# A two-layer encoder kernel: order of the opening, a neighbourhood table laid out in full, and Hyena loads and PSUM reads moved

## The chip, the cores and the metric

One core of a Trainium2 chip runs the whole kernel in one launch. The metric is device time in microseconds (us) of one execution. PE is the matmul engine, DVE the vector engine, ACT the scalar engine, POOL the GpSimd engine, SP the engine whose queue issues most loads; ACT and POOL can issue transfers too.

## The reference

Input x is 512 tokens of 1024 channels, in float32, and so is the output. Each of two layers computes x + post_norm(mixer(pre_norm(x))) and then x + post_norm(ffn(pre_norm(x))), the norms being RMS norms:

```python
def rms_norm(x, gain):
    y = x * lax.rsqrt(jnp.mean(x * x, axis=-1, keepdims=True) + EPS)
    return y * gain
# mixer, layer 0: 8 heads of latent attention beside 8 heads of 2-D neighbourhood attention
#   s = q.k_window * scale + rpb[row_off][:, col_off];  p = softmax(s);  o = p.v_window
# mixer, layer 1: 4 heads of retention (forward and backward) beside 512 Hyena channels
#   z = dwconv3(u_proj);  x0, x1, v = split(z);  u = v * x1
#   y = irfft(rfft(u, 2L) * rfft(k_circ, 2L))[:L] + u * hy_bias;  out = y * x0
def conv_ffn(h, w_gate, w_up, conv_w, w_down):
    return (gelu(dwconv3(h @ w_gate, conv_w)) * (h @ w_up)) @ w_down
```

The neighbourhood table rpb is indexed by the offset between a query and each key of its 8 by 16 window; keys outside of the window take no part.

## The kernel before

**Arithmetic.** Activations lie channel-major: 8 tiles of 128 channels x 512 tokens. Every operand of a product is split into a high part in float32r and the rest (`split_to`, line 273: a cast on ACT, a subtraction on DVE or POOL), and `mm` (line 278) makes three matmuls of two parts each. A weight piece is 128 x 1024: `load_weight` (line 250) has SP load it to one of 2 `raw` buffers, ACT cast it to `whi` and DVE subtract to `wlo` (4 buffers each). `weight_ahead` keeps three pieces ahead of the one in use. PSUM has 8 banks in four tags: pj (2), A (3), B (2), C (1).

**Order.** The program is written in one order (`main`, line 522), and a planner then issues each engine's instructions by its own model of the times: of those that are ready in the model the first in program order goes first; `high_priority(n)` moves a block up by n places, and `issue_after(ins)` keeps a block behind `ins` on that instruction's engine. Each engine and each of the queues SP, ACT and POOL then runs its list strictly in order. A tile's memory is handed on when its last reader is done; a phase (l0, f0, l1, f1) takes over the memory of the one before, in the order in which its tags are first used.

**Opening.** 16 warm-up products of ones (line 528); SP loads x and the first four weight pieces in turn. Line 539 scales and splits x tile by tile (`scaled`, line 331), with a square on ACT (line 542) and a running sum on POOL (line 544) after each tile. `proj_tok` (line 476) makes the values of the neighbourhood heads: 8 steps over the channels, 12 matmuls each; before step 5 `stats` (line 286: sum over partitions on PE, then a power on POOL), before step 6 `spread` and a copy to `Rb`; `loads` (line 564) comes before step 7 and has SP load the column mask, the table rpb (8 x 384 columns, without mask) and the rope table. The four results are read from PSUM by ACT (line 598) and DVE (line 599).

**Neighbourhood heads, then latent heads.** `na0` (line 622) makes q and k and adds rpb and mask to three bias tiles per head (line 631, DVE); `na1` scores and softmax, `na2` transposes and values. `latent_kv` makes the rope part of the keys, kr (lines 728 to 731). `parts` (line 736), between the heads' last stages, splits kr three times into `kall` (line 746, ACT and POOL), which takes over the memory of rpb. Then `ml0`, `ml1`, `ml2` run pipelined.

**Boundary** (line 339): the output product, post norm, residual and next pre norm, in two halves of 256 tokens; the last four weight columns' products of the next stage run over the halves (`proj_halves`). Its two `stats` end in a power on POOL, and at its end `rcol`, spread to `Rb` (line 447).

**Layer 1.** The ffn of layer 0 also makes the Hyena filters (`filters`, line 963) and stores them to DRAM (`filt`, line 1004). `mixer1` (line 1061) stores x to DRAM (line 1065), has POOL load the forward transform's matrices (`dft_consts`, line 930), and runs `conv` for 12 projections through one tile `cv`: the first four read the products `pre` that the boundary left in PSUM. `spectrum` (line 1008) loads the filters back by ACT's queue, splits them and transforms them, in steps between the projections. The transform of u and the products with the filters follow (lines 1113 to 1143, chiefly DVE), then `proj_tok` for the retention values (read from PSUM by `scaled`, line 1149), three `gate` projections (line 1106, read by DVE), and the inverse transform (line 1162). `decays` (line 1040) is a chain of some 25 operations on 128 x 8 elements.

Of the kernel before, what the change touches and what calls it, by code (L numbers as in the profile page):

```python
# [16 lines left out]
P = 128  # L17
# [26 lines left out]
def shape_constants():  # L44
# [18 lines left out]

    mask = np.zeros((P, 3, 32, GR), np.float32)
    for typ, (q0, k0) in enumerate(((0, 0), (16, 8), (48, 32))):
        for p in range(P):
            col = q0 + p // GR
            st = min(max(col - 8, 0), GW - 16)
            kc = k0 + np.arange(32)
            mask[p, typ, (kc < st) | (kc >= st + 16), :] = -1.0e30  # L70
    c["namask"] = f32(mask.reshape(P, 3 * 256))
# [41 lines left out]
def lay_out(inp):  # L113
# [78 lines left out]

    r = np.pad(inp["a_rpb"][0], ((0, 0), (0, 0), (16, 16)))
    q = np.arange(P)
    r = r[:, 7 - (q % GR)[:, None, None] + np.arange(GR)[None, None, :], 15 - (q // GR)[:, None, None] + np.arange(48)[None, :, None]]
    a["rpb"] = f32(r.transpose(1, 0, 2, 3).reshape(P, MH * 384))
# [9 lines left out]
class Body:  # L206
    def __init__(self, ctx, tc, I, out, dbg=None):
# [10 lines left out]
        self.filt = self.dp.tile([2, S, HC], F32, name="filt")  # L218
        self.n = 0
        self.wi = 0  # L220
        self.wq = []
        self.cols = self.cp.tile([P, NCOL], F32, name="cols")
# [27 lines left out]
    def load_weight(self, n=1):  # L250
# [4 lines left out]
        for i in range(n):  # L255
            c = slice(i * 1024 // n, (i + 1) * 1024 // n)
            nc.sync.dma_start(raw[:, c], self.I["w"][self.wi][:, c])
            with self.tc.high_priority(WP):
                nc.scalar.copy(hi[:, c], raw[:, c])  # L259
                nc.vector.tensor_tensor(lo[:, c], raw[:, c], hi[:, c].bitcast(F32), ALU.subtract)  # L260
# [78 lines left out]
    def boundary(self, pool, tag, x, prod, gpost, gpre, ns, ftag, perm=False, rin=None):  # L339
# [104 lines left out]
        with self.tc.issue_after(self.last_mm):  # L444
            with self.tc.high_priority(HP):
                self.stats([acc2], D, out=self.rcol)
            nc.scalar.copy(self.Rb, self.spread(self.rcol, "C"))
# [74 lines left out]
    def main(self):  # L522
# [14 lines left out]
        with self.phase("l0") as p:  # L537
            acc = None
            for k in range(KT):
                self.scaled(h[k], x[k], self.col(C_MPRE + k), slice(0, S))  # L540
                sq = self.X("sq", tag="xb")
                nc.scalar.activation(sq, x[k], AF.Square)
                if acc is not None:
                    nc.gpsimd.tensor_tensor(acc, acc, sq, ALU.add)
                else:
                    acc = sq
            x, h, pre = self.mixer0(p, h, acc)
# [10 lines left out]
    def mixer0(self, p, h, acc):  # L558
        nc = self.nc
        mask = p.tile([P, 3 * 256], F32, name="namask")  # L560
        rope = p.tile([P, 2, S], F32, name="rope0")
        big = p.tile([P, MH, 384], F32, tag="big", name="rpb")

        def loads():
            nc.sync.dma_start(mask, self.I["namask"])
            for hd in range(0, MH, 2):
                nc.sync.dma_start(big[:, hd:hd + 2], self.I["rpb"][:, hd * 384:hd * 384 + 768].rearrange("p (a b) -> p a b", a=2))
            nc.sync.dma_start(rope, self.I["rope0"].rearrange("p (a b) -> p a b", a=2))
# [13 lines left out]
        def value_mm(ops, v, hd, pt, start, stop):  # L582
# [6 lines left out]
        pss = self.proj_tok(h, {7: loads, 5: lambda: self.stats([acc], D, out=self.rcol),  # L589
                                6: lambda: nc.scalar.copy(self.Rb, self.spread(self.rcol))})  # L590
# [31 lines left out]
        def na0(hd, _):  # L622
# [5 lines left out]
            b = p.tile([P, 2, 256], F32, tag="bias", bufs=2, name=self.nm("bias"))  # L628
            b = [b[:, 0], b[:, 1], self.X("bias", tag="xb")[:, :256]]
            for t, o in enumerate((128, 64, 0)):  # L630
                nc.vector.tensor_tensor(b[t], big[:, hd, o:o + 256], mask[:, t * 256:t * 256 + 256], ALU.add)
            return b
# [90 lines left out]
        def latent_kv():  # L723
# [8 lines left out]
            lat["kr"] = kr  # L732
# [3 lines left out]
        def parts():  # L736
# [7 lines left out]
            kall = p.tile([P, 6, S], F32R, tag="big", name="kall")  # L744
            for i in range(3):
                self.split_to(kall[64:128, 2 * i], kall[64:128, 2 * i + 1], lat["kr"][64:128], nc.gpsimd)
# [122 lines left out]
    def ffn(self, p, x, h, pre, l):  # L869
# [18 lines left out]
        for j in range(FT):  # L888
# [5 lines left out]
            nc.vector.tensor_tensor(t, gps, Rb, ALU.mult)  # L894
# [35 lines left out]
    def dft_consts(self, p, name):  # L930
        out = []
        for i, part in enumerate(("hi", "lo")):
            t = p.tile([P, 4, 2, 256], F32R, tag="dft" + part, name=name + part)
            self.nc.gpsimd.dma_start(t.rearrange("p m a b -> p (m a b)"), self.I[name][:, i * 2048:(i + 1) * 2048])
# [28 lines left out]
    def filters(self, new):  # L963
# [28 lines left out]
        for tk in range(4):  # L992
# [10 lines left out]
            for i, src in enumerate((t, n)):  # L1003
                nc.sync.dma_start(self.filt[i, ts], src)
# [3 lines left out]
    def spectrum(self, mats, at, kt, spec):  # L1008
        nc = self.nc
        for par in range(2):  # L1010
            for trig in range(2):
                m = 2 * par + trig
                sd = []
                for hh in range(2):
                    t = self.X("sd", tag="xb")
                    tk = 2 * par + hh
# [3 lines left out]
                for ft in range(2):  # L1020
                    ps = self.PS("C")
                    for hh in range(2):
                        c = slice(ft * P, ft * P + P)
                        self.mm(ps, (mats[0][:, m, hh, c], mats[1][:, m, hh, c]), sd[hh], hh == 0, hh == 1)
                    if par == 0:
                        t = self.X("sp", tag="xb")
                        nc.scalar.activation(t, ps, AF.Copy, scale=1.0 / 512)
                        spec[ft, trig] = t
                    else:
                        e, o, d = spec[ft, trig], kt(), kt()  # L1030
# [266 lines left out]
```

## Time and profile before

| | |
|---|---|
| median of 3 runs (each) | 1312.72 us (1308.06, 1312.72, 1312.88) |
| the profiled execution: time, span | 1307.53 us, 1305.8 us |
| PE busy (share of the span) | 1271.7 us (97%) |
| DVE, ACT, POOL busy | 813.9 (62%), 582.9 (45%), 80.9 us (6%) |
| mean granted clock of PE | 0.993 |

The span runs from the first to the last instruction. Busy time of an engine is the union of its instructions; an average over stages hides where an engine stands idle, so the stages are looked at one by one. The granted clock is the share of full speed that the throttle let PE have.

### The profile page before, as it was taken

To read this page: it belongs to the slowest core of one execution; us is meant where nothing else is said; L and a number is where in the kernel's file an instruction comes from. 1 tells how busy PE (TensorE), PEld (TensorE's weight loads), DVE (VectorE), ACT (ScalarE), POOL (GpSimd) and SP (SyncE) were. 2 spreads that over 40 slices of the span, in tenths; PEclk is the share of its full clock that TensorE was granted. 3 is DMA by queue.
4 is the path that set the end of the run, shared out by engine and by line. 5 is a ranking of instruction groups with operands and counts; after the bars stand their busy time and mean duration, and the time that the engine had idled before them with its cause. 6 is when DMAs were issued, how large, how long until landed. Compare 5 with 4: busy or idle time off the path is not lost.

```text
span 1305.8 us, 16380 instructions
## 1 busy us (share of the span) xinstructions
PE 1271.7 (97%) x6370; PEld 1057.5 (81%) x6370; DVE 813.9 (62%) x1298; ACT 582.9 (45%) x943; POOL 80.9 (6%) x73
## 2 busy tenths in 40 slices
PE   9999799999999999999999999999999999999997
PEld 7788677997888788888987878778988888888886
DVE  6679898478766665322588785774875555552223
ACT  5456798456533333222454245544653333332221
POOL 4021322000000000000000000000000000000002
PEclk9999899999999999999999989999999999999999
DMA  7222012223434333333264233214233333333331
GB/s 269 86 65 79 3 33 68 82 79 116 121 123 135 122 113 97 99 111 97 83 226 128 58 120 95 81 49 130 66 113 98 97 97 97 97 97 104 107 97 65
DMA packets 41563, 130.62 MB, mean 100 GB/s; under 512 B 4652, under 2 KB 6892, under 8 KB 40973
## 3 DMA queue, kind: packets, MB, share of 16 engines
q1 hardware_dynamic: 35868, 116.92, 29.0%
q10 hardware_dynamic: 5040, 8.45, 2.0%
q0 software_dynamic: 576, 4.19, 0.9%
q8 instruction: 50, 0.82, 0.3%
q14 instruction: 29, 0.23, 0.1%
HBM read 123.26 MB, written 6.29 MB: 99 GB/s over the span
## 4 chain that ended last, share of the span: by engine, by line
PE 87%; DVE 5%; ACT 3%; issue 2%; DMA 1%; POOL 1%; SPq 0%; DVEq 0%; POOLq 0%; ACTq 0%
PE pspj L280 17%; PE pspj L282 17%; PE pspj L281 17%; PE psA L280 10%; PE psA L282 10%; PE psA L281 10%; DVE wlo L260 1%; ACT e L794 1%; DMA raw<-in_w 1%; PE psB L292 1%; PE psB L671 1%; PE psB L810 1%; DVE h L334 1%; ACT whi L259 1%; PE psC L282 1%
## 5 line engine op out<-in xcount | busy, mean ns | idle before, releaser
L259 ACT CAST whi<-raw 128x1024 fp32r<-128x1024 f32 (+1 forms) x200 | 209.1, 1048 | 432.1 <-PE pspj L281 237.8
L260 DVE TENSOR_TENSOR wlo<-raw,whi 128x1024 fp32r<-128x1024 f32 (+1 forms) x200 | 246.6, 1235 | 204.8 <-ACT whi L259 202.8
L280 PE MATMUL pspj<-h,whi 128*128 128x512 f32 (+1 forms) x664 | 250.5, 377 | 2.8 <-DVE v L599 2.7
L281 PE MATMUL pspj<-h,whi 128*128 128x512 f32 (+1 forms) x664 | 249.6, 376 | 0.0
L282 PE MATMUL pspj<-h,wlo 128*128 128x512 f32 (+1 forms) x664 | 249.4, 376 | 0.0
L282 PE MATMUL psA<-h,wlo 128*128 128x512 f32 (+1 forms) x424 | 155.4, 367 | 0.7 <-DVE wlo L260 0.7
L280 PE MATMUL psA<-h,whi 128*128 128x512 f32 (+1 forms) x424 | 156.1, 368 | 0.0
L281 PE MATMUL psA<-h,whi 128*128 128x512 f32 (+1 forms) x424 | 155.1, 366 | 0.0
L280 PEld LDWEIGHTS pspj<-h,whi 128*128 128x128 f32 x664 | 125.5, 189 | 25.4 <-DVE v L599 3.1
L282 PEld LDWEIGHTS pspj<-h,wlo 128*128 128x128 f32 x664 | 125.4, 189 | 22.2
L281 PEld LDWEIGHTS pspj<-h,whi 128*128 128x128 f32 x664 | 125.5, 189 | 22.0
L280 PE MATMUL pspj<-ahi,whi 128*128 128x512 f32 x308 | 121.4, 394 | 0.0
L282 PE MATMUL pspj<-ahi,wlo 128*128 128x512 f32 x308 | 120.7, 392 | 0.0
L281 PE MATMUL pspj<-alo,whi 128*128 128x512 f32 x308 | 119.5, 388 | 0.0
L282 PEld LDWEIGHTS psA<-h,wlo 128*128 128x128 f32 x424 | 79.8, 189 | 15.5 <-DVE wlo L260 1.9
L280 PEld LDWEIGHTS psA<-h,whi 128*128 128x128 f32 x424 | 80.0, 189 | 14.8 <-issue 2.6
L281 PEld LDWEIGHTS psA<-h,whi 128*128 128x128 f32 x424 | 80.0, 189 | 12.4
L894 DVE TENSOR_TENSOR t<-psA,Rb 128x512 f32<-128x512 f32 x40 | 27.6, 691 | 83.4 <-PE psA L282 83.3
L282 PEld LDWEIGHTS pspj<-ahi,wlo 128*128 128x128 f32 x308 | 57.8, 188 | 13.5
L281 PEld LDWEIGHTS pspj<-alo,whi 128*128 128x128 f32 x308 | 57.8, 188 | 12.9
L280 PEld LDWEIGHTS pspj<-ahi,whi 128*128 128x128 f32 x308 | 57.9, 188 | 11.5
L299 POOL TENSOR_TENSOR r<-v,mhalf 128x2 f32<-128x2 f32 (+1 forms) x14 | 13.7, 977 | 847.7 <-DVE v L297 690.2
(360 smaller groups left out, 2140.1 us busy)
## 6 DMA issues: line engine op xcount, KB each, us to landing
raw<-in_w SPq DMA_DIRECT2D x198, 512.0 KB, 3.5
x<-in_xT SPq DMA_DIRECT2D x16, 256.0 KB, 4.8
fflt<-in_fwin SPq DMA_DIRECT2D x8, 256.0 KB, 2.9
xspill<-f ACTq DMA_DIRECT2D x8, 256.0 KB, 2.6
sd<-filt ACTq DMA_DIRECT2D x8, 256.0 KB, 3.3
x<-xspill ACTq DMA_DIRECT2D x8, 256.0 KB, 3.2
rpb<-in_rpb SPq DMA_DIRECT2D x4, 384.0 KB, 4.6
filt<-fs SPq DMA_DIRECT2D x4, 256.0 KB, 2.5
```

What stands on the lines that cost most here:

```text
L259: nc.scalar.copy(hi[:, c], raw[:, c])
L260: nc.vector.tensor_tensor(lo[:, c], raw[:, c], hi[:, c].bitcast(F32), ALU.subtract)
L280: nc.tensor.matmul(ps, stat[0], mov[0], start=start, stop=False)
L281: nc.tensor.matmul(ps, stat[0], mov[1], start=False, stop=False)
L282: self.last_mm = nc.tensor.matmul(ps, stat[1], mov[0], start=False, stop=stop).ins
L292: nc.tensor.matmul(ps[:, j:j + 1], a[:, j * P:(j + 1) * P], self.ones, start=a is accs[0], stop=a is accs[-1])
L299: self.pow = nc.gpsimd.tensor_tensor(r, v, self.mhalf[:, :c], ALU.pow)
L334: self.nc.vector.scalar_tensor_tensor(lo, src, g, hi.bitcast(F32), ALU.mult, ALU.subtract)
L671: tr = lambda o, i: nc.tensor.transpose(o, i, self.ident)
L794: nc.scalar.activation(e, ps, AF.Exp, bias=nmx, accum_out=den[:, i:i + 1])
L810: nc.tensor.transpose(pt[:, i * P:(i + 1) * P], es[i][:, j * P:(j + 1) * P], self.ident)
L894: nc.vector.tensor_tensor(t, gps, Rb, ALU.mult)
```

## The change

1. *Opening.* All eight tiles are scaled and split before the squares; the running sum goes from POOL to DVE; `stats` and the copy to `Rb` come one step later; 14 warm-up products instead of 16. The rope table is loaded by POOL's queue, in program order after `proj_tok`.
2. *Neighbourhood table.* The host lays rpb out with the mask in it (8 heads x 3 kinds x 256 columns, 3 MB in place of 1.5 MB and a mask of 0.4 MB); each head's bias tile (three buffers) is loaded by POOL's queue, and the additions on DVE are gone.
3. *kr* is split into `kall` where it is made; `kall` has memory of its own.
4. *Boundaries.* Casts of weight pieces that come later in the program stay behind the copy to `Rb` on ACT.
5. *Hyena.* The filters are split before they are stored (twice the bytes); POOL's queue loads the parts, all 16 tiles at once behind the matrices of the transform, whose load is put 300 places up; the tiles x0 come first in the phase's memory; the four products `pre` are read into x0 at once; x is stored to DRAM after the second `conv`; `decays` runs in the ffn before; the gate projections and the retention values are read from PSUM by ACT alone.

```diff
 opening (main), and mixer0
-            acc = None
             for k in range(KT):
                 self.scaled(h[k], x[k], self.col(C_MPRE + k), slice(0, S))
-                sq = self.X("sq", tag="xb")
-                nc.scalar.activation(sq, x[k], AF.Square)
-                if acc is not None:
-                    nc.gpsimd.tensor_tensor(acc, acc, sq, ALU.add)
...
+            sqs = [self.X("sq", tag="xb") for _ in range(KT)]
+            for k in range(KT):
+                nc.scalar.activation(sqs[k], x[k], AF.Square)
+                if k:
+                    nc.vector.tensor_tensor(sqs[0], sqs[0], sqs[k], ALU.add)
...
-            nc.sync.dma_start(mask, self.I["namask"])
...
-            nc.sync.dma_start(rope, self.I["rope0"].rearrange("p (a b) -> p a b", a=2))
+            nc.gpsimd.dma_start(rope, self.I["rope0"].rearrange("p (a b) -> p a b", a=2))
...
-            for t, o in enumerate((128, 64, 0)):
-                nc.vector.tensor_tensor(b[t], big[:, hd, o:o + 256], mask[:, t * 256:t * 256 + 256], ALU.add)
+            b = p.tile([P, 3, 256], F32, tag="bias", bufs=3, name=self.nm("bias"))
+            nc.gpsimd.dma_start(b, self.I["rpb"][:, hd * 768:hd * 768 + 768].rearrange("p (a b) -> p a b", a=3))
...
-            lat["kr"] = kr
+            for i in range(3):
+                self.split_to(kall[64:128, 2 * i], kall[64:128, 2 * i + 1], kr[64:128], nc.gpsimd)
 load_weight, boundary
+                with self.tc.issue_after(self.hold) if self.hold is not None else ExitStack():
+                    nc.scalar.copy(hi[:, c], raw[:, c])
...
+            self.hold = nc.scalar.copy(self.Rb, self.spread(self.rcol, "C")).ins
 ffn
+            if l == 0 and j == 4:
+                with self.tc.issue_after(scaled.ins):
+                    self.decay = self.decays(self.cp)
 filters, spectrum
-                nc.sync.dma_start(self.filt[i, ts], src)
+                hl = self.X("fh", F32R), self.X("fl", F32R)
+                self.split_to(*hl, src)
+                for part in range(2):
+                    nc.sync.dma_start(self.filt[part, i, ts], hl[part].bitcast(F32))
...
-                    nc.scalar.dma_start(t, self.filt[trig, tk * P:(tk + 1) * P])
-                    sd.append(at(trig))
-                    self.split_to(*sd[-1], t)
+                    with self.tc.high_priority(300), self.tc.issue_after(self.consts):
+                        nc.gpsimd.dma_start(parts[m][hh][part], self.filt[part, m % 2, tk * P:(tk + 1) * P])
 mixer1
-        for k in range(KT):
-            nc.scalar.dma_start(spill[k * P:(k + 1) * P], x[k])
-        mats = self.dft_consts(p, "dftf")
+        x0 = [p.tile([P, S], F32, name=f"x0{j}") for j in range(4)]
+        with self.tc.high_priority(300):
+            mats = self.dft_consts(p, "dftf")
...
+        for j in range(4):
+            scaled(pre[j], x0[j])
...
+            if j == 1:
+                with self.tc.issue_after(self.taken):
+                    for k in range(KT):
+                        nc.scalar.dma_start(spill[k * P:(k + 1) * P], x[k])
...
-            g, ps = self.X("rg", tag="xb"), self.proj(h)
-            nc.vector.tensor_tensor(g, ps, Rb, ALU.mult)
+            g = self.X("rg", tag="xb")
+            nc.scalar.copy(g, self.proj(h))
+            nc.vector.tensor_tensor(g, g, Rb, ALU.mult)
...
+            t = self.X("rv", tag="xb")
+            nc.scalar.activation(t, ps, AF.Copy, scale=rcol[:, j:j + 1])
             rv.append(two("t1"))
-            self.scaled(rv[-1], ps, rcol[:, j:j + 1], slice(0, S))
+            self.split_to(*rv[-1], t)
...
-        lg = self.decays(p)
+        lg = self.decay
```

## Rows read from the trace of the kernel before

**Rows 1.** The page, busy time of each engine, its share of the span, instructions.

```profile
PE 1271.7 (97%) x6370; PEld 1057.5 (81%) x6370; DVE 813.9 (62%) x1298; ACT 582.9 (45%) x943; POOL 80.9 (6%) x73
```

**Rows 2.** Four stretches: length, PE, PEld, DVE, ACT, POOL busy, PEclk, DMA share, GB/s.

```profile
35.00:165.00 130.00, 123.17 (x639) 99.53 (x638) 104.36 (x204) 73.93 (x168) 24.76 (x18) 0.97 0.19 57
...
128.00:154.00 26.00, 19.20 (x91) 14.36 (x92) 21.32 (x45) 16.56 (x43) 8.78 (x7) 0.87 0.07 20
...
296.00:640.00 344.00, 344.00 (x1547) 280.85 (x1547) 189.81 (x272) 128.88 (x160) 0.70 (x1) 1.00 0.36 111
...
766.00:780.00 14.00, 10.99 (x45) 9.08 (x44) 11.87 (x17) 5.13 (x8) 0.00 (x0) 0.76 0.37 114
```

**Rows 3.** Timeline of PE in the opening: start, length, line, operands, idle before it.

```profile
0.93 6.51 PE L528 MATMUL psC<-ones 128*128 128x128 f32 x32 [0.93 <-DVE ones L226]
...
19.61 0.50 PE L281 MATMUL pspj<-wlo,h 128*128 128x512 f32 x1 [1.03 <-DVE wlo L260]
...
34.69 0.50 PE L280 MATMUL pspj<-h,whi 128*128 128x512 f32 x1 [2.71 <-DVE v L599]
```

**Rows 4.** Timeline of ACT, DVE and POOL in the opening.

```profile
31.67 1.05 ACT L259 CAST whi<-raw 128x1024 fp32r<-128x1024 f32 x1 [3.49 <-DMA raw<-in_w]
...
7.49 0.75 DVE L334 SCALAR_TENSOR_TENSOR h<-x,cols,h 128x512 fp32r<-128x512 f32 x1
...
12.12 5.20 DVE L334 SCALAR_TENSOR_TENSOR h<-x,cols,h 128x512 fp32r<-128x512 f32 x3
...
11.63 9.08 POOL L544 TENSOR_TENSOR sq<-sq,sq 128x512 f32<-128x512 f32 x5 [0.52 <-ACT sq L542]
```

**Rows 5.** Timeline of SP's queue in the opening.

```profile
12.60 0.43 SPq L565 DMA_DIRECT2D namask<-in_namask  x1
...
19.59 0.33 SPq L257 DMA_DIRECT2D raw<-in_w  x1
```

**Rows 6.** Loads of line 257 issued between 668 and 690, issue to landing.

```profile
DMA to landing us min/median/max: 3.5/4.5/6.8
```

**Rows 7.** Timeline from 118 to 141: ACT, POOL, DVE and PE.

```profile
133.53 1.66 ACT L274 CAST kall<-kr 64x512 fp32r<-64x512 f32 x3
...
134.22 3.76 POOL L275 TENSOR_TENSOR kall<-kr,kall 64x512 fp32r<-64x512 f32 x3 [9.52 <-ACT kall L274]
...
118.07 0.61 DVE L665 TENSOR_SCALAR ebuf<-ebuf,rd 128x256 f32<-128x256 f32 x2
...
131.46 0.41 DVE L631 TENSOR_TENSOR bias<-rpb,namask 128x256 f32<-128x256 f32 x1
...
139.28 1.68 DVE L665 TENSOR_SCALAR ebuf<-ebuf,rd 128x256 f32<-128x256 f32 x2
...
139.41 0.48 PE L671 MATMUL psB<-ident,s 128*128 128x128 f32 x2 [2.99 <-DVE s L665]
```

**Rows 8.** Timeline at the head of layer 1: POOL and PE.

```profile
645.50 1.08 POOL L299 TENSOR_TENSOR r<-v,mhalf 128x2 f32<-128x2 f32 x1 [8.04 <-DVE v L297]
...
670.48 0.76 POOL L934 DMA_DIRECT2D dftfhi<-in_dftf  x1 [23.91 <-ACT t L274]
...
680.10 0.50 PE L282 MATMUL psC<-t,dftflo 128*128 128x512 f32 x1 [2.24 <-DMA dftflo<-in_dftf]
...
698.64 0.50 PE L1101 MATMUL psB<-ident,u 128*128 128x128 f32 x2 [1.26 <-DVE u L1090]
```

**Rows 9.** Line 275 on POOL, head outputs: count, ns min/median/max, first and last start.

```profile
L275 POOL TENSOR_TENSOR a<-at,a x15: 1270/1295/2142, 68.0 to 223.8; 64x512 fp32r<-64x512 f32 x15
```

**Rows 10.** Timeline from 765 to 775: ACT, DVE and PE.

```profile
765.03 0.69 ACT L333 ACTIVATE t<-pspj,rcol 128x512 fp32r<-128x512 f32 x1 [1.79 <-PE pspj L282]
...
773.41 0.74 DVE L334 SCALAR_TENSOR_TENSOR t<-pspj,rcol,t 128x512 fp32r<-128x512 f32 x1
...
769.45 0.38 PE L280 MATMUL psA<-dftihi,t 128*128 128x256 f32 x1 [1.78 <-ACT t L274]
...
774.54 0.63 PE L280 MATMUL pspj<-h,whi 128*128 128x512 f32 x1
```

More of the change, by code (lines that the diff above doesn't have):

```diff
@@ L194, in lay_out @@
     q = np.arange(P)
-    r = r[:, 7 - (q % GR)[:, None, None] + np.arange(GR)[None, None, :], 15 - (q // GR)[:, None, None] + np.arange(48)[None, :, None]]
-    a["rpb"] = f32(r.transpose(1, 0, 2, 3).reshape(P, MH * 384))
+    t = np.full((P, MH, 3, 32, GR), -1.0e30, np.float32)
+    for typ, (q0, k0) in enumerate(((0, 0), (16, 8), (48, 32))):
+        col, kc = q0 + q // GR, k0 + np.arange(32)
+        off = (16, 8, 0)[typ] + np.arange(32)
+        e = r[:, 7 - (q % GR)[:, None, None] + np.arange(GR)[None, None, :], 15 - (q // GR)[:, None, None] + off[None, :, None]]
+        st = np.minimum(np.maximum(col - 8, 0), GW - 16)[:, None]
+        near = (kc[None, :] >= st) & (kc[None, :] < st + 16)
+        t[:, :, typ] = np.where(near[:, None, :, None], e.transpose(1, 0, 2, 3), t[:, :, typ])
+    a["rpb"] = f32(t.reshape(P, MH * 768))
     fw = np.zeros((P, 64 + 64 + 64 + 1024), np.float32)
@@ L588, in mixer0 @@
         self.new_factor()
-        pss = self.proj_tok(h, {7: loads, 5: lambda: self.stats([acc], D, out=self.rcol),
-                                6: lambda: nc.scalar.copy(self.Rb, self.spread(self.rcol))})
+        pss = self.proj_tok(h, {6: lambda: self.stats([acc], D, out=self.rcol),
+                                7: lambda: nc.scalar.copy(self.Rb, self.spread(self.rcol))})
+        loads()
         rcol, Rb = self.rcol, self.Rb
@@ L627, in na0 @@
                 pair[hd // 2] = q, qk_tile(kn)
[L628 to L632 removed]
+            b = p.tile([P, 3, 256], F32, tag="bias", bufs=3, name=self.nm("bias"))
+            nc.gpsimd.dma_start(b, self.I["rpb"][:, hd * 768:hd * 768 + 768].rearrange("p (a b) -> p a b", a=3))
+            return [b[:, t] for t in range(3)]
         def na1(hd, bias):
@@ L1084, in mixer1 @@
                               lambda: p.tile([P, S], F32, tag="t2", bufs=8, name=self.nm("ks")), ks)
-        u, x0 = [], [p.tile([P, S], F32, name=f"x0{j}") for j in range(4)]
+        next(steps)
         for j in range(4):
-            u.append(conv(8 + j, p.tile([P, S], F32, name=f"u{j}")))
+            scaled(pre[j], x0[j])
+        u = []
+        for j in range(4):
+            u.append(conv(8 + j, p.tile([P, S], F32, name=f"u{j}"), x0[j]))
+            if j == 1:
+                with self.tc.issue_after(self.taken):
+                    for k in range(KT):
+                        nc.scalar.dma_start(spill[k * P:(k + 1) * P], x[k])
         for j in range(4):
@@ L1264 @@
 WP = 5
-WARM = 16
+WARM = 14
 LATE = 7
```

88 lines of the change are left out of this document (38 added, 50 removed).

## The prediction

> **What bounds the kernel now.** The page comes first: PE is busy for 97% of the span and no other engine for more than 62% [rows 1]. The kernel is bound by its matmuls, and the change removes none of them but two warm-ups. What can be won is the 34 us in which PE stands idle, and the time in which it runs at the lower of its clocks. So I asked next for busy time by stretches. In the ffn of layer 0 PE is busy for 344.00 of 344.00 us [rows 2]: whatever the change puts there costs nothing while DVE (189.81) and ACT (128.88) have room. Between 35 and 165 us PE loses 6.83 us, and nearly all of it (6.80) between 128 and 154 [rows 2]. Between 766 and 780 it loses 3.01 us more. In both stretches the granted clock falls, to a mean of 0.87 and 0.76; elsewhere it is 1.00. Then I read the timelines where PE waits: the opening [rows 3, 4], the passage from neighbourhood to latent heads [rows 7], the head of layer 1 [rows 8] and the gates [rows 10].
>
> **Opening.** PE waits 1.03 us for a low part of a weight at 19.61 and 2.71 us at 34.69 for the values to be read from PSUM [rows 3]. The first wait comes from DVE: its split takes 0.75 us alone, but three take 5.20 while POOL's sums run (five in 9.08) [rows 4]. With the sums on DVE that stretching ends. The second wait is that ACT, due to read PSUM, stood 3.49 us at a weight still in flight [rows 4], issued behind the tables on SP's queue [rows 5]; without tables there it comes earlier. Two warm-ups fewer are 4 of 32 records in 6.51 us, so 0.8 us [rows 3]. Together up to 4.5 us. Late next would be the second weight piece. For the tables do not stay behind: the planner issues what is ready. The mask left SP at 12.60, the fifth weight piece at 19.59, though that piece comes first in the program [rows 5]. Rope and the first three bias tiles wait for nothing, and POOL has nothing else to do, so I expect those four loads (1.7 MB by their shapes) within the first 5 us, beside x and the first weights. Beside 2.1 MB that POOL loaded in layer 1 a weight took up to 6.8 us to land, where the quickest took 3.5 [rows 6]. So 1.7 MB delay a piece by 3.3 x 1.7 / 2.1 = 2.7 us. I take 2.0 us as the gain; the ends are 4.5 (no collision) and -0.9 (two pieces delayed).
>
> The Trainium skill, "DMA: Bandwidth & Descriptors", section "Issuing engines are not separate DMA queues", says that transfers run on the same 16 engines and interleave whichever engine issued them, so that another queue saves only the issuing time. By that rule the tables would push the loads back by their whole volume and the opening would win about nothing: a median of 1299.7 instead of the 1297.7 below. The delay in rows 6 agrees in kind; a queue to queue share is not shown by any row.
>
> **Neighbourhood table.** 24 additions at 0.41 us [rows 7], 9.8 us of DVE, go. They lie where PE waits for nothing but the stretch counted next: nothing. The eight loads on POOL's queue wait for the tile three heads back; what is queued behind them is POOL's splits of head outputs, wanted only at the output product. Nothing.
>
> **kr.** Between 128 and 154 the late chain is softmax, transposes, PE. ACT spends 1.66 us on three casts of kr in its middle, and POOL's 3.76 us of subtractions beside it stretch two products on DVE from 0.61 to 1.68 [rows 7]. Both leave the stretch: 1.66 + 1.07 = 2.7 us off the wait of 2.99 at 139.41. With that wait gone PE should keep its clock; 0.13 x 26 = 3.4 us of full speed were lost [rows 2], part of it in idle time, so I count 2.3. Sum 5.0, ends 0 (another order of ACT brings the wait back) and 9.1 (all idle time and the clock). Where kr is made now, before 128, PE has no wait to lengthen.
>
> **Boundaries.** The casts held back are of pieces that have no free buffer before the copy anyway: nothing either way, within half a us.
>
> **Head of layer 1.** POOL's load of the transform stood until 670.48, and PE waited 2.24 us for it at 680.10 [rows 8]. The matrices' memory was that of the boundary's sums. With the x0 tiles in front they take over split activations, dead when the last down product ends, which is before the power at 645.50 [rows 8], so this wait goes. DVE loses eight splits and the `decays` chain in this stretch, ACT eight casts and a change of tables; the wait of 1.26 for u [rows 8] should shrink. I count 2.24 + 0.8 = 3.0. Ends: 4.3 (both waits and the idle of the first part) and -2.0 for the new: 18 loads now stand in POOL's queue at the very time of the boundary's two powers, the first at 645.50 [rows 8]. Two issues ahead of a power cost 2 x 0.76 us. The moved splits and `decays` land in the ffn under its 344 us of PE; if that cover were gone they would cost eight splits at about 0.74 us (the nearest row, [rows 10]) and the small chain, some 10 us. The stores of x leave ACT's queue where nothing waits for them. Nothing.
>
> **Values and gates.** At 765.03 ACT reads the first value bank, DVE at 773.41 only, as its products with the filters stand in front [rows 10]. So the first gate's matmul comes at 774.54, and PE takes inverse transforms instead, whose inputs are late (1.78 us at 769.45 and more) [rows 10]. Read by ACT alone the bank is free near 766, a gate follows at once, and three gates of 24 matmuls each give DVE time to catch up. The idle 3.0 us and the lost clock, 0.24 x 14 = 3.4 us [rows 2], make 6.4. I take 5.0, as ACT gets four casts and three copies more; ends 0 and 6.4, below nothing by 1 if ACT falls behind.
>
> **Sum.** 2.0 + 5.0 + 3.0 + 5.0 = 15.0 us. The profiled execution took 1307.53 us for a span of 1305.8, so it would take 1292.5. The runs' median stands 5.2 us higher, at 1312.72; the same gain puts it at 1297.7.
>
> **Rivals.**
> - *The planner puts the inverse transform first again.* It works with model times, and nothing forces gates first. For it: it did so before. Against it: in the model too the bank is free sooner. That term is 0, and the time 1302.7.
> - *The waits pass on.* DVE is busy for 21.32 of 26 us around the passage and 11.87 of 14 us at the gates [rows 2]. If it is the next to be late, two thirds of the gains come back as other waits: 5 us are left, 1307.7. Nearly no change.
> - *POOL's queue becomes the path.* At the boundary before layer 1 all 18 loads are ready when the last down product ends, shortly before the power at 645.50. If they go first, the power waits 18 x 0.76 = 13.7 us, or, stretched beside DVE as POOL's subtractions were (2142 against 1270 ns) [rows 9], 23 us. The second half of the products hangs on that power through spread, update and splits, with little to cover it, so PE would stand some 22 us. Against it: the power has a place of higher rank than the loads. It decides when more than some ten issues get in front. The other terms are 12, so the time is 1312.7 + 22 - 12 = 1322.7: slower.
>
> The Trainium skill, "SBUF — State Buffer", section "SBUF: two separate sides", warns that POOL cannot write descriptors while DVE runs an operation that takes their shared port pair, so that a load issued by POOL looks blocked by DVE; with its figure of about 3.1 us in place of 0.62 us, 18 issues would be an estimated 56 us. No row here shows such an issue.
>
> **How the numbers follow.** Two runs of this kernel differ by less than about 0.5% (6.6 us) with nothing changed; faster is below 1306.1, slower above 1319.3. Chances: forecast 0.50 (1289 to 1304), inverse first 0.13, waits pass on 0.25, POOL's queue 0.12. Faster is 0.50 + 0.13 + a fifth of 0.25 = 0.68, same 0.20, slower 0.12. The lower end takes the upper bounds (4.5 + 9.1 + 4.3 + 6.4 = 24.3, so 1288.4) and 2 us for the runs' spread: 1286. The upper end takes in the passed-on waits with the same spread and a bit: 1312. POOL's queue stays out.
>
> **What would show it.** Opening: splits of 0.75 us on DVE throughout, the product of queries near 32 instead of 34.69, and the table loads on POOL before 5 us. Passage: no idle of 3 us near 139, clock 1.00. Head of layer 1: the transform loaded near 645, no wait for it. Gates: three gate products right behind the values, clock 1.00 between 766 and 780. The prediction is wrong if PE's busy share stays at 97%, if waits of PE for DVE appear instead, or if the boundary near 645 grows by over 5 us.

## The result, and the profile after

The kernel after takes 1296.08 us (median of 4 runs, 1294.92 to 1297.54); the kernel before 1312.1 us (median of 4 runs, 1308.06 to 1312.88). The ratio is 0.9885 with a 95% interval of 0.9862 to 0.9908: faster by some 1.2%. The profiled execution took 1295.89 us for a span of 1294.1, so 11.64 us less than before's, where the sum of the prediction said 15.0.

The page of the kernel after, busy time of each engine, beside [rows 1]:

```profile
PE 1268.4 (98%) x6366; PEld 1055.1 (82%) x6366; DVE 803.0 (62%) x1281; ACT 587.3 (45%) x951; POOL 81.6 (6%) x91
```

PE's busy time fell by 3.3 us and its idle time by 8.4; DVE lost 10.9, ACT gained 4.4. To see where, both traces are cut at the same events: the first product of queries, POOL's split of the last neighbourhood head's output, the second power of the boundary before layer 1, POOL's load of the inverse transform, the first power behind it, the last power. The stretches of the kernel before (columns as in [rows 2]):

```profile
34.69:160.04 125.35, 118.52 (x614) 95.95 (x615) 100.01 (x196) 70.13 (x159) 22.28 (x16) 0.97 0.20 59
...
160.04:645.50 485.46, 483.63 (x2413) 398.40 (x2413) 295.26 (x466) 230.18 (x368) 21.76 (x19) 1.00 0.32 98
...
645.50:748.00 102.50, 96.78 (x519) 81.56 (x518) 85.20 (x156) 45.66 (x72) 3.80 (x5) 1.00 0.41 134
748.00:842.58 94.58, 91.57 (x434) 76.08 (x433) 69.44 (x105) 45.74 (x65) 3.61 (x4) 0.96 0.32 100
842.58:1297.36 454.78, 450.69 (x2256) 379.96 (x2254) 235.30 (x336) 170.70 (x252) 11.99 (x13) 1.00 0.30 93
```

and of the kernel after, with the ffn of layer 0 as a last row:

```profile
34.28:160.52 126.24, 120.11 (x614) 96.25 (x615) 92.61 (x176) 70.57 (x160) 24.52 (x22) 0.97 0.25 75
...
160.52:645.91 485.39, 483.56 (x2413) 398.46 (x2413) 303.38 (x500) 236.56 (x378) 21.71 (x18) 1.00 0.33 103
...
645.91:743.26 97.35, 95.50 (x519) 82.00 (x518) 77.20 (x122) 39.84 (x62) 11.67 (x21) 1.00 0.49 162
743.26:830.59 87.33, 87.33 (x432) 73.19 (x431) 69.23 (x105) 49.69 (x73) 3.68 (x5) 1.00 0.34 108
830.59:1285.38 454.79, 450.71 (x2258) 379.88 (x2256) 235.19 (x336) 170.77 (x252) 11.96 (x12) 1.00 0.30 93
...
296.00:640.00 344.00, 344.00 (x1545) 280.45 (x1544) 198.03 (x306) 135.34 (x170) 0.70 (x1) 1.00 0.38 117
```

| stretch | before | after | gained | forecast |
|---|---|---|---|---|
| opening, to the first product of queries | 34.69 | 34.28 | 0.41 | 2.0 |
| heads and passage | 125.35 | 126.24 | -0.89 | 5.0 |
| to the boundary before layer 1 | 485.46 | 485.39 | 0.07 | 0 |
| head of layer 1 | 102.50 | 97.35 | 5.15 | 3.0 |
| values, gates, inverse transform | 94.58 | 87.33 | 7.25 | 5.0 |
| rest | 454.78 | 454.79 | -0.01 | 0 |

All of the gain is in layer 1. The first two terms, 7 of the 15 us, won nothing together. The work moved into the ffn raised DVE there from 189.81 to 198.03 us, and PE still had no gap.

The opening in the timeline of the kernel after (POOL, SP's queue, ACT, PE), beside [rows 3 to 5]:

```profile
1.29 0.76 POOL L564 DMA_DIRECT2D rope<-in_rope  x1 [0.35 <-issue]
...
2.39 1.65 POOL L626 DMA_DIRECT2D bias<-in_rpb  x3
...
9.69 0.33 SPq L257 DMA_DIRECT2D raw<-in_w  x1
...
10.79 0.72 ACT L335 ACTIVATE h<-x,cols 128x512 fp32r<-128x512 f32 x1 [1.86 <-DMA x<-in_xT]
...
11.56 0.69 PE L282 MATMUL pspj<-whi,h 128*128 128x512 f32 x1 [2.06 <-ACT h L335]
...
34.28 0.50 PE L282 MATMUL pspj<-h,whi 128*128 128x512 f32 x1 [0.35 <-DVE v L596]
```

The tables go out in the first 4 us, as forecast. ACT then splits the second x tile at 10.79 us (6.74 before). The wait of 2.71 at the product of queries is down to 0.35, but PE now waits 2.06 us for that x tile, and then the granted clock falls, as the windows view from 12 to 24 us shows (columns as in [rows 2]):

```profile
12.00:24.00 12.00, 12.00 (x48) 9.53 (x47) 11.95 (x17) 9.67 (x16) 0.00 (x0) 0.87 0.64 227
```

Where kr is split now, in the timeline of the kernel after (ACT, POOL, DVE, PE):

```profile
78.87 1.65 ACT L276 CAST kall<-kr 64x512 fp32r<-64x512 f32 x3 [1.37 <-POOL kr L726]
...
79.56 2.25 POOL L277 TENSOR_TENSOR kall<-kr,kall 64x512 fp32r<-64x512 f32 x1 [0.73 <-ACT kall L276]
...
82.94 0.39 PE L580 MATMUL psA<-phi,v 128*128 128x256 f32 x1 [1.31 <-ACT phi L276]
...
83.25 1.84 DVE L660 TENSOR_SCALAR s<-s,rd 128x256 f32<-128x256 f32 x1
...
86.27 0.39 PE L581 MATMUL psA<-plo,v 128*128 128x256 f32 x1 [0.62 <-DVE plo L277]
```

The three casts stand ahead of a softmax on ACT, and one normalisation on DVE takes 1.84 us beside POOL's subtractions (0.34 for the same operation at 85.54). PE, without a gap there before, waits twice.

The head of layer 1 in the timeline of the kernel after (POOL, PE), beside [rows 8]:

```profile
645.91 1.07 POOL L301 TENSOR_TENSOR r<-v,mhalf 128x2 f32<-128x2 f32 x1 [8.04 <-DVE v L299]
646.94 0.60 POOL L930 DMA_DIRECT2D dftfhi<-in_dftf  x1
...
653.36 0.54 POOL L1016 DMA_DIRECT2D t<-filt  x1 [2.11 <-DMA dftfhi<-in_dftf]
...
671.92 1.03 POOL L301 TENSOR_TENSOR rcol<-v,mhalf 128x4 f32<-128x4 f32 x1 [8.89 <-DVE nlg L1197]
...
677.08 0.50 PE L282 MATMUL psC<-t,dftfhi 128*128 128x512 f32 x1 [0.67 <-ACT Rb L449]
```

The transform goes out at 646.94 instead of 670.48, behind the second power, and POOL is done with all 18 loads 8.89 us before the third.

The values and gates in the timeline of the kernel after (ACT, PE), beside [rows 10]:

```profile
760.29 0.69 ACT L1162 ACTIVATE rv<-pspj,rcol 128x512 f32<-128x512 f32 x1 [1.77 <-PE pspj L284]
...
762.07 0.39 PE L282 MATMUL pspj<-h,whi 128*128 128x512 f32 x1
```

The first gate's product follows ACT's first read by 1.78 us (9.51 before), and PE has no gap in the whole stretch.

### The profile page after: what moved, and what is told of

Same layout as the page of the kernel before. It is cut to its first block, busy times and chain, and to the rows that moved or that the text cites. A ratio compares the mean times of both kernels' runs of the same rounds, so it can differ in the third digit from the quotient of the medians.

```text
span 1294.1 us, 16436 instructions
## 1 busy us (share of the span) xinstructions
PE 1268.4 (98%) x6366; PEld 1055.1 (82%) x6366; DVE 803.0 (62%) x1281; ACT 587.3 (45%) x951; POOL 81.6 (6%) x91
## 4 chain that ended last, share of the span: by engine, by line
PE 86%; ACT 3%; DVE 2%; issue 2%; POOL 1%; POOLq 0%; DVEq 0%; ACTq 0%
PE pspj L282 16%; PE pspj L284 16%; PE pspj L283 16%; PE psA L282 11%; PE psA L284 10%; PE psA L283 10%; ACT e L787 1%; PE psB L294 1%; PE psB L803 1%; PE psC L282 1%; PE psC L283 1%; POOL r L301 1%; PE psC L284 1%; ACT whi L261 0%; PE psB L666 0%
## 5 line engine op out<-in xcount | busy, mean ns | idle before, releaser
L262 DVE TENSOR_TENSOR wlo<-raw,whi 128x1024 fp32r<-128x1024 f32 (+1 forms) x200 | 243.7, 1220 | 215.5 <-ACT whi L261 213.7
```

## The experiments

Each ratio is to the kernel before, run beside the variant. Medians of variants that ran at different times differ by 1 to 3 us by chance as well (the kernel before had medians of 1312.1, 1309.82, 1308.95, 1309.02 and 1309.1), so the verdicts rest on the stretches of the profiled executions. "The distance" below is that from the first product of queries to POOL's split of the last neighbourhood head's output; the expectations call that split the first latent head's, which is a slip of mine.

### Opening: where the tables stand

**Tables behind x** (e1_tables_behind), after with:

```diff
+            self.late = nc.gpsimd.tensor_copy(self.small(1, "late"), x[KT - 1][:, :1]).ins
...
-            nc.gpsimd.dma_start(rope, self.I["rope0"].rearrange("p (a b) -> p a b", a=2))
+            with self.tc.issue_after(self.late):
+                nc.gpsimd.dma_start(rope, self.I["rope0"].rearrange("p (a b) -> p a b", a=2))
...
-            nc.gpsimd.dma_start(b, self.I["rpb"][:, hd * 768:hd * 768 + 768].rearrange("p (a b) -> p a b", a=3))
+            with self.tc.issue_after(self.late):
+                nc.gpsimd.dma_start(b, self.I["rpb"][:, hd * 768:hd * 768 + 768].rearrange("p (a b) -> p a b", a=3))
```

> The kernel after, with one edit: POOL copies one column of the last x tile and the rope and bias loads stay behind that copy. My theory: the 1.7 MB of tables, sent beside x, delayed x and the first weights (the second x tile is split at 10.79 us instead of 6.74) and ate the opening's gain, so here the second split comes back to about 6.7 us, the product of queries starts near 32 us instead of 34.28, and the median is 2 to 4 us below the kernel after (1292 to 1294). Rival: the opening is bound by the volume that all loads move together, or by the readers of PSUM; then the product of queries stays within 0.7 us of 34.3 and the time within 1 us of the kernel after.

Median 1293.17 us, ratio 0.9863 (0.9843 to 0.9882). The second split is at 7.36 us, the product of queries at 32.21. My theory stands, the rival falls.

**Tables behind the power** (e7_tables_pow), the same holds, with:

```diff
-        loads()
+        self.late = self.pow.ins
...
+            if hd == 2:
+                loads()
```

> The kernel after, with the first three bias loads held behind POOL's power (near 25 us) and the rope load behind them; no copy is added. My theory: at 17 us, where the first trial put them, the tables still stood in the way of the fifth and sixth weight pieces (ACT waited 4.06 and 3.93 us there); held further back they delay nothing that is wanted before 47 us, where the first bias is read. So the second split is near 6.7 to 7.4 us, the product of queries near 31 to 32, the median 1292 to 1293. Rival: the weight pieces come at the pace of their two buffers (load, cast, subtraction) and not of the transfers; then the product of queries stays at 32.2 and nothing is won against the first trial (1293.2).

Median 1291.88 us, ratio 0.9877 (0.9862 to 0.9892). In the timeline of this kernel (ACT, POOL, PE):

```profile
6.77 0.72 ACT L335 ACTIVATE h<-x,cols 128x512 fp32r<-128x512 f32 x1 [0.25 <-DMA x<-in_xT]
...
25.28 1.83 POOL L628 DMA_DIRECT2D bias<-in_rpb  x3
...
30.23 0.50 PE L282 MATMUL pspj<-h,whi 128*128 128x512 f32 x1 [0.20 <-DVE v L597]
```

and in its windows view:

```profile
12.00:24.00 12.00, 12.00 (x59) 10.09 (x58) 9.18 (x14) 7.64 (x11) 0.00 (x0) 1.00 0.48 160
```

The product of queries is 2.0 us earlier than in the first trial and 4.05 earlier than in the kernel after. The opening itself was worth 34.69 - 30.23 = 4.46 us, nearly the 4.5 that the prediction gave as the end without a collision; the early tables took it back. In the eight profiled executions with the tables first, that product started at 33.39 to 34.85, mean 34.03, so the early tables cost 3 to 4 us (3.8 by this run, 3.1 by the 30.93 of e11_combined below). The loads of x took a median of 8.7 us to land in the kernel after and 5.8 here. PE made 59 products from 12 to 24 us here and 48 in the kernel after. The fallen clock belongs to that one execution: in the other seven with the tables first the mean clock of the opening was 1.00, and the product came no earlier.

### Passage: where kr stands, and the additions

**kr back in program order** (e2_kr_back), the split moved back from `latent_kv` to `parts`:

```diff
-            for i in range(3):
-                self.split_to(kall[64:128, 2 * i], kall[64:128, 2 * i + 1], kr[64:128], nc.gpsimd)
+            lat["kr"] = kr
...
+            for i in range(3):
+                self.split_to(kall[64:128, 2 * i], kall[64:128, 2 * i + 1], lat["kr"][64:128], nc.gpsimd)
             lat["kall"] = kall
```

> The kernel after, with kr split in the passage again, as before the change, while kall keeps its own memory. My theory: moving kr moved a wait and took none away. So PE's two waits near 83 and 86 us (1.31 and 0.62) go, the q latents' power on POOL comes back from 115.80 to about 113.8, the wait of about 3 us near 139 returns, and the progress mark at the first head output of the latent heads (160.52 in the kernel after) moves by less than 1 us either way; the median stays within 1 us of 1296. Rival: the move did win its 2.7 us and something else near 80 us lost it; then that mark comes 2 to 3 us later and the median is 1298 to 1299.

Median 1294.94 us, ratio 0.9876 (0.9854 to 0.9898). A miss: the splits stayed at 78.75 us, since the planner issues what is ready. What had held them at 133 us in the kernel before was the memory that `kall` took over from the table, not their place. The run does not tell the theories apart.

**kr held in the passage** (e5_kr_passage), `self.put` being ACT's copy of the head's output (in `put_out`), the split gone from `latent_kv`:

```diff
             stage(na, na2, 2, NAH[i - 2])
+            for n in {7: (0, 1, 2)}.get(i, ()):
+                with self.tc.issue_after(self.put):
+                    self.split_to(kall[64:128, 2 * n], kall[64:128, 2 * n + 1], lat["kr"][64:128], nc.gpsimd)
```

> The kernel after, with the three splits of kr held on ACT behind the copy of head 5's output, so that they stand in the passage as before the change (putting them back in program order alone had left them near 79 us). My theory: the move only moved a wait. So PE's waits near 83 and 86 us go, PE waits about 3 us near 139 again, and from the first product of queries to POOL's split at the first latent head (125.1 us in three of the runs of the kernel after and its variants, 125.35 before) the time stays within 1 us; the median is within 1.5 us of 1296. Rival: the move won its 2.7 us and the clock of the passage, and something else in the change lost them; then that distance grows by 2 us or more and the median is 1298 or above.

Median 1296.3 us, ratio 0.9904 (0.9889 to 0.9919). In the timeline of this kernel (ACT, POOL, PE):

```profile
133.42 1.65 ACT L276 CAST kall<-kr 64x512 fp32r<-64x512 f32 x3
...
134.18 3.76 POOL L277 TENSOR_TENSOR kall<-kr,kall 64x512 fp32r<-64x512 f32 x3 [8.85 <-ACT kall L276]
...
139.47 0.66 PE L666 MATMUL psB<-ident,s 128*128 128x128 f32 x2 [1.40 <-DVE s L660]
```

The waits near 83 and 86 are gone, the one at 139 is back (1.40, with one of 1.43 ahead of it). The distance is 126.36. Over all profiled executions it is 125.03 to 127.06 with kr in the passage (four, mean 125.95) and 124.31 to 126.24 with kr early (eight, mean 125.42). So the move is worth some 0.5 us at most, less than the spread between executions, and not 5.0.

**kr taken apart** (e6_kr_spread), against e5_kr_passage:

```diff
-            for n in {7: (0, 1, 2)}.get(i, ()):
+            for n in {4: (0,), 5: (1,), 6: (2,)}.get(i, ()):
                 with self.tc.issue_after(self.put):
-                    self.split_to(kall[64:128, 2 * n], kall[64:128, 2 * n + 1], lat["kr"][64:128], nc.gpsimd)
+                    self.split_to(kall[64:128, 2 * n], kall[64:128, 2 * n + 1], lat["kr"][64:128], nc.vector)
```

> The kernel after, with kr's three splits taken apart: each held on ACT behind the output copy of another neighbourhood head (2, 3, 4), and subtracted on DVE, not on POOL. My theory: at 79 us the casts stood in the way of a softmax on ACT (1.65 us) and POOL's subtractions stretched DVE's normalisation; one cast at a time fits between, so the waits near 83 and 86 us (1.9 us) go, the distance named above shrinks by 1 to 2 us, and the median is near 1294.5. Rival: PE is paced by the chain of each head's softmax wherever kr stands; then the waits come up elsewhere before 155 us and the distance stays within 0.5 us.

Median 1293.75 us, ratio 0.9886 (0.987 to 0.9903). One of ACT's three casts in the timeline of this kernel, and its windows view over the distance:

```profile
96.28 0.62 ACT L276 CAST kall<-kr 64x512 fp32r<-64x512 f32 x1
```

```profile
33.39:156.51 123.12, 118.67 (x614) 95.61 (x615) 93.92 (x179) 71.06 (x160) 19.80 (x18) 0.99 0.25 77
```

The casts stand at 96.28, 106.23 and 121.46 us, PE waits nowhere near 83, and the distance is 2.3 us shorter than that mean, 123.12. So the waits near 83 and 86 were kr's doing, and this edit takes them away instead of moving them: PE's idle time in the distance is 4.45 us, where the eight have 6.11 to 7.25. The edit both spreads the splits and moves their subtractions from POOL to DVE; the two were not tried apart.

**Additions put back** (e4_adds_back), in `na0`:

```diff
+        zero = p.tile([P, 256], F32, name="zero")
+        nc.vector.memset(zero, 0.0)
...
+            for t in range(3):
+                nc.vector.tensor_tensor(b[:, t], b[:, t], zero, ALU.add)
             return [b[:, t] for t in range(3)]
```

> The kernel after, with the 24 additions of 128x256 on DVE put back (the bias tiles get a tile of zeros added; the result does not change). My theory, as in the prediction: DVE has room for 9.8 us of additions between 35 and 130 us, so taking them out won nothing and putting them back costs under 1 us. Rival: with the kr splits now in that stretch the additions were what made room for them; then the waits near 83 us grow, a new wait comes up before 126, and the median rises by 2 to 5 us.

Median 1296.73 us, ratio 0.9897 (0.9876 to 0.9917); distance 125.16. No new wait: the additions were free.

### Head of layer 1: memory and POOL's queue

**x0 behind the matrices** (e8_x0_late):

```diff
-        x0 = [p.tile([P, S], F32, name=f"x0{j}") for j in range(4)]
         with self.tc.high_priority(300):
             mats = self.dft_consts(p, "dftf")
...
+        x0 = [p.tile([P, S], F32, name=f"x0{j}") for j in range(4)]
         next(steps)
```

> The kernel after, with the memory of the four x0 tiles given out after the matrices of the transform, as before the change. My theory, as in the prediction: what freed the transform's load was the memory that it takes over. So its load stands again until about 670 us, with the 16 filter loads behind it, PE waits 2 us or more for the transform near 680 and more for the filters, and the stretch from the boundary's second power (645.9) to the inverse transform's load (743.3) grows from 97.4 to 101 or more; the median is 1299 to 1302. Rival: the raised place of the load in the planner freed it; then the load stays at 647 and the median within 1 us of 1296.

Median 1311.22 us, ratio 1.0016 (1.0007 to 1.0026): the whole gain of the change is gone. In the timeline of this kernel (POOL, PE), and its windows view:

```profile
669.77 0.60 POOL L930 DMA_DIRECT2D dftfhi<-in_dftf  x1 [23.82 <-ACT whi L261]
...
676.34 0.53 POOL L1016 DMA_DIRECT2D t<-filt  x1 [2.26 <-DMA dftfhi<-in_dftf]
...
686.93 1.03 POOL L301 TENSOR_TENSOR rcol<-v,mhalf 128x4 f32<-128x4 f32 x1
...
688.02 1.12 PE L318 MATMUL psC<-ident,rcol 128*128 128x128 f32 x4 [13.09 <-POOL rcol L301]
```

```profile
644.88:758.65 113.77, 98.84 (x519) 84.16 (x518) 77.10 (x122) 39.95 (x62) 11.70 (x21) 0.92 0.42 139
...
680.00:690.00 10.00, 1.31 (x5) 0.91 (x6) 0.21 (x1) 0.83 (x2) 5.46 (x10) 0.50 1.27 395
```

My theory had the place right and the price far too low. The load waits for memory until 669.77, all 18 loads stand ahead of the boundary's last power, and it comes 17.2 us after the first of them, 15.0 later than in the kernel after. PE waits 13.09 us for it and then runs at a granted clock of 0.50. The stretch is 113.77 us instead of 97.35. This is the prediction's rival "POOL's queue becomes the path"; in the kernel after only the order of the memory keeps it away. The raised place of the load, which this kernel has too, does not free it alone; whether the order of the memory would do without it was not tried.

**The two lines alone** (e12_before_x0), on the kernel before:

```diff
-        mats = self.dft_consts(p, "dftf")
+        x0 = [p.tile([P, S], F32, name=f"x0{j}") for j in range(4)]
+        with self.tc.high_priority(300):
+            mats = self.dft_consts(p, "dftf")
...
-        u, x0 = [], [p.tile([P, S], F32, name=f"x0{j}") for j in range(4)]
+        u = []
```

> The kernel before, with two lines of the change alone: the x0 tiles come first in the memory of layer 1, and the transform's load is put 300 places up. The filters stay unsplit and on ACT's queue. My theory: this alone takes the transform's waits (0.53 and 2.24 us) away, the rest of the head's gain (the waits for the spectrum and for u) came from the lighter DVE and ACT. So the load goes out near 646 us, the stretch from the boundary's second power (645.50) to the inverse transform's load (748.00) falls from 102.5 us by 2.5 to 3.2, and the waits of 0.69 and 1.26 stay; the median is near 1306. Rival: the convolutions' loads and casts run behind DVE anyway, and the transform's wait passes on to u; then the stretch shrinks by less than 1 us. If the granted clock falls with the wait in some executions, as it did with the same wait in the trial of the gates alone (0.66 for 10 us), the gain is larger than 3.2.

Median 1305.98 us, ratio 0.998 (0.9963 to 0.9998). The transform is loaded at 646.80, and the spectrum's and u's waits stay, as expected. In the timeline of this kernel (ACT, PE):

```profile
676.41 1.04 ACT L259 CAST whi<-raw 128x1024 fp32r<-128x1024 f32 x1 [1.22 <-DMA raw<-in_w]
677.36 0.58 ACT L447 COPY Rb<-psC 128x512 f32<-128x512 f32 x1
...
677.99 0.50 PE L280 MATMUL psC<-t,dftfhi 128*128 128x512 f32 x1 [1.72 <-ACT Rb L447]
```

But the stretch shrank by 1.67 us (645.75 to 746.58), not by 2.5 to 3.2: a weight cast ahead of the copy to `Rb` on ACT took over as a wait of 1.72. In the kernel after that cast is held behind the copy, and the wait is 0.67. So the hold at the boundaries, which the prediction put at nothing, seems to let the transform's gain through here; the hold alone was not tried.

### Values and gates

**DVE reads again** (e3_gates_dve):

```diff
-            g = self.X("rg", tag="xb")
-            nc.scalar.copy(g, self.proj(h))
-            nc.vector.tensor_tensor(g, g, Rb, ALU.mult)
+            g, ps = self.X("rg", tag="xb"), self.proj(h)
+            nc.vector.tensor_tensor(g, ps, Rb, ALU.mult)
...
-            t = self.X("rv", tag="xb")
-            nc.scalar.activation(t, ps, AF.Copy, scale=rcol[:, j:j + 1])
             rv.append(two("t1"))
-            self.split_to(*rv[-1], t)
+            self.scaled(rv[-1], ps, rcol[:, j:j + 1], slice(0, S))
```

> The kernel after, with the gate projections and the retention values read from PSUM by DVE as well, as before the change; all else stays. My theory: this part alone took away the stall of the gates, so PE is idle for about 3 us between 755 and 785 again at a lower granted clock, and the stretch from the inverse transform's load to the first power after it (87.3 us in the kernel after, 94.6 before) is 6 to 7 us longer; the median is about 1302.5. Rival: the x0 tiles read at once and the lighter DVE behind the head of layer 1 took the stall away; then PE stays busy there and the median rises by less than 2 us.

Median 1301.65 us, ratio 0.9931 (0.9913 to 0.995). The stretch in the windows view of this kernel, and its stall in the timeline of PE:

```profile
741.84:835.03 93.19, 90.18 (x434) 75.17 (x433) 68.88 (x105) 45.74 (x65) 3.68 (x5) 0.98 0.32 101
```

```profile
763.31 0.39 PE L282 MATMUL psA<-dftihi,t 128*128 128x256 f32 x1 [1.78 <-ACT t L276]
764.47 0.39 PE L284 MATMUL psA<-dftihi,t 128*128 128x256 f32 x1 [0.65 <-DVE t L277]
765.67 0.58 PE L284 MATMUL psA<-dftihi,t 128*128 128x256 f32 x1 [0.58 <-DVE t L277]
```

The stretch grows by 5.86 us, a little less than expected, with the same three waits as before. The theory stands.

**Only the gates read by DVE** (e9_values_act): the first half of that diff alone.

> The kernel after, with only the three gate projections read from PSUM by DVE again; the retention values stay with ACT. My theory: what opened the way was that the value banks are read without DVE, so the first gate's product follows the first ACT read by under 2 us (760.29 and 762.07 in the kernel after). DVE then reads each finished gate some us late at most, with two banks to wait in. So no idle time between 755 and 785, and the median within 1 us of 1296. Rival: the gates' own reads matter as much; then the second or third gate waits for DVE, PE takes the inverse transform in between, and 2 us or more of the 5.6 us that undoing both cost come back (1298 or above).

Median 1297.11 us, ratio 0.9911 (0.9892 to 0.993). The stretch is 87.91 us, without a gap. So 5.3 of the 5.9 us hang on who reads the values, not on who reads the gates.

**This part on the kernel before** (e10_before_gates): that diff turned round, on the kernel before.

> The kernel before, with one part of the change alone: gate projections and retention values read from PSUM by ACT. My theory: this part does not hang on the others, so the stall of 3.0 us near 770 and its lost clock go here too, the stretch from the inverse transform's load to the first power behind it falls from 94.6 us to 87 to 89, and the median is 5 to 7 us below the kernel before. Rival: in the kernel before, DVE also has the decay chain and later filter work near there and ACT its Silu tables; then the wait passes on and the gain is under 2 us.

Median 1304.58 us, ratio 0.9962 (0.9946 to 0.9977); stretch 87.30 us in the windows view of this kernel:

```profile
751.85:839.15 87.30, 87.30 (x432) 73.19 (x431) 69.59 (x105) 49.78 (x73) 3.61 (x5) 1.00 0.34 108
...
680.00:690.00 10.00, 8.80 (x26) 7.04 (x27) 7.46 (x17) 3.04 (x5) 0.00 (x0) 0.66 0.50 177
```

The part stands on its own: 7.28 us of the stretch. The median fell by 4.4, a little less than expected; in the profiled execution 2.7 us were lost at the head of layer 1, where the clock fell to 0.66 behind a wait for the transform of 2.26.

### Both improvements together

(e11_combined): the diffs of e7_tables_pow and e6_kr_spread, on the kernel after.

> The kernel after with both edits that won: the tables held behind POOL's power, and kr's splits taken apart, held behind the output copies of heads 2 to 4 and subtracted on DVE. My theory: the two stretches do not touch, so the gains add: the product of queries near 30.2 us, the distance from there to the first latent head's split 123.1 instead of 125.4, and the median 2 us below the 1291.9 of the tables alone, near 1289.8. Rival: with the tables late the bias tiles or rope arrive late for the heads, or the passage takes the same time wherever it starts; then 1291 to 1292.

Median 1289.43 us, ratio 0.9851 (0.9831 to 0.987), the lowest of all. The product of queries starts at 30.93 and the distance is 123.15: the gains add, and this version beats both kernels.

## Why the prediction was right and wrong

The time came out 1.6 us below the forecast, but largely by chance, for errors cancelled. Two terms of 7.0 us together brought -0.48, the two others, of 8.0, brought 12.40. So the sum was 3.4 us too high for the profiled execution, and the 5.2 us by which before's median stood over its profiled execution did not carry over: after's median stands 0.2 over its own. Of the signs that it named, two did not come: the product of queries near 32 (34.28) and a clock of 1.00 in the passage (0.50 between 139 and 144).

- *Opening, 2.0 forecast, 0.41 measured.* The mechanism was right: DVE's splits take 0.75 us each, the tables go out first and delay the loads. The term was mis-sized: "3.3 x 1.7 / 2.1 = 2.7 us" for one piece. The tables delayed the second x tile by 4 us and cost 4.05 us at the product of queries (e7_tables_pow; 3 to 4 over all executions), by a wait of PE for x and, in this execution, a lower clock behind it. The Trainium skill's rule that I had set against it ("DMA: Bandwidth & Descriptors", section "Issuing engines are not separate DMA queues") gave about nothing, and the trace agrees: 0.41, with x's loads landing in a median of 8.7 us beside the tables and 5.8 without.
- *Additions at nothing.* Right, by e4_adds_back.
- *kr, 5.0 forecast, -0.89 measured.* The step that failed is "Where kr is made now, before 128, PE has no wait to lengthen." PE had no gap there, but no slack behind it either: 1.65 us of casts ahead of one softmax, and DVE stretched beside POOL, made 1.93 us of waits, and the neighbourhood heads came late to the passage. There other waits stood (1.50 for `qf`, 1.38 for `phi`). The clock did not bring the 2.3 us either. Its mean over the distance stayed at 0.97 here; in six of the eight executions with kr early it was 0.99 or 1.00, and the distance was still 124.31 to 125.58, for PE's idle time in it (6.11 to 7.25 us over the eight) was no shorter than with kr in the passage (6.07 to 6.90). This is the rival "waits pass on", in this one stretch.
- *Boundaries at nothing.* Right up to 645 us. At the head of layer 1 probably not: in e12_before_x0, which lacks the hold, a cast ahead of `Rb` makes a wait of 1.72; in the kernel after it is 0.67.
- *Head of layer 1, 3.0 forecast, 5.15 measured.* The transform's waits went, for the reason given (memory), which e8_x0_late shows. The term of 0.8, for the wait of 1.26 for u, was too small: the wait for u went whole, the spectrum's fell from 0.69 to 0.46. Idle time explains 3.87 of the 5.15 (5.72 to 1.85); in the other 1.28 the same 519 matmuls came at shorter distances, and which of the lighter engines did that was not tried apart.
- *Values and gates, 5.0 forecast, 7.25 measured.* Right in mechanism. The 1.4 us held back for ACT's added work were not needed: ACT was never late. The windows make it 3.01 of idle time and 4.24 of PE's busy time, most of it the clock (0.96 over 94.58 us is some 3.8), against 6.4 in the prediction's upper end.
- *POOL's queue.* It did not come, but it was nearer than a chance of 0.12 suggests: one allocation order decides it. The prediction put it ahead of the second power at 22 us; where it came, it was ahead of the third, and 16.4 us of the stretch.
- *Inverse first* did not come; e3_gates_dve shows that it does as soon as DVE reads the values.

## What to carry to other kernels

With a planner such as this one, a load or a split that waits for nothing is issued when it is ready, not where the program has it: hold it behind an instruction that comes when its cover is there. A stretch where the bound engine has no gap is not free for other engines; look at the chain that feeds it, and try small pieces apart rather than all at once. Before putting many issues on a queue, look at what else that queue carries: here one power behind 18 loads was worth the whole change.

## What was not expected of the hardware

- POOL's queue took eight loads at once, and the ninth only when the first had landed (653.36 in the kernel after, 676.34 in e8_x0_late). So the 18 loads took 16.1 us, though one issue takes 0.53. The trace has a semaphore instruction on POOL's sequencer for 15 of the 16 filter loads, so the limit may be the program's and not the chip's; what sets it was not tried.
- A wait for the transform of the same length, 2.24 and 2.26 us, left the granted clock at 1.00 in the kernel before and dropped it to 0.66 over 10 us in e10_before_gates. So a wait's cost in clock cannot be read from its length alone.
- The Trainium skill, "SBUF — State Buffer", section "SBUF: two separate sides", warns that POOL cannot write descriptors while DVE runs an operation in a two-port mode. The prediction's estimate of 56 us for 18 issues did not come true: from 645.5 to 660 us DVE was busy for 14.50 of 14.50 us, with `tensor_tensor` and `scalar_tensor_tensor` operations, and the 16 filter loads took 0.527 to 0.607 us each to issue. Whether any of these operations runs in that mode no run here shows, so the warning is neither confirmed nor refuted.
